# Residual loads of finished rows brought forward a tile, and the first low parts of the second pass put in front of subtractions

## The chip, the cores and the metric

The kernel runs on one core of one Trainium2 chip. Its time is the device time of one execution in microseconds (us), and the lower the better. The kernel before takes 2166.55 us, the median of three runs (2166.4 to 2170.19). In the profile the engines are PE (TensorE, matrix products; PEld is its loading of weights), DVE (VectorE), ACT (ScalarE), POOL (GpSimd) and SP (SyncE, which here issues nearly all DMA transfers).

## The reference, cut to what matters

One decoder layer is computed for 2048 prompt rows and 64 sample rows of width 1024: attention and gated linear attention side by side, an output projection, and then an MLP. The change touches the MLP alone:

```python
h = rms_norm(x, g_ffn_pre)
u = jax.nn.relu(jnp.einsum('btd,df->btf', h, w_up))      # 1024 -> 4096
f = jnp.einsum('btf,fd->btd', u * u, w_down)             # 4096 -> 1024
x = x + rms_norm(f, g_ffn_post)
```

So each row ends with a norm of `f`, a multiplication by the gain `g_ffn_post`, and the addition of the residual `x` (called `x1` in the kernel, kept in DRAM as `x1_d`).

## The kernel before

**Passes.** The MLP is worked in two passes (`sb` 0 and 1) of 1024 prompt rows each; the sample rows go with the first. A pass is first 16 "up units" (`up`, one for each 256 columns of the hidden width, `fc` 0 to 15), which leave the squared features in DRAM (`s_d`), and then the down products (`down`). Then the second pass does the same.

**Down products.** The product with `w_down` is done by a scheme of seven products in place of eight, each half as large in both directions. `DOWN_ORDER` has them as 6, 1, 5, 3, 2, 7, 4. Each product runs over 16 chunks of the hidden width, so a pass has 7 x 16 units `(p, fc)`. Sums of weights and features for the products lie ready in DRAM, in `s_d` and `t_d` (or are read from `w_down` itself).

**A unit.** A unit takes a feature tile (letter s, loaded as `rs`) and a weight tile (letter t, loaded as `rt`), 128 x 512 each. Both are split in two so that the fast matrix product keeps full precision (`split_copy`, L226 to L229): ACT copies the raw tile to a rounded high part (`o0s`, `o0t`, L228), DVE subtracts it from the raw tile and so gets the low part (`o1s`, `o1t`, L229). PE then does 12 matmuls, three for each of four row tiles: high t with high s, low t with high s, high t with low s (into banks `dn`). The unit's very first matmul needs only high parts; its second is the first that needs `o1t`.

**Places and look-ahead.** In the first pass raw tiles and parts have three places each (in the second four for the raw tiles and five for the parts). `load` issues the two raw transfers three units ahead on SP's queue; a transfer waits until the place is free, that is until DVE has made the low part of the unit three before.

**Finishing rows.** When product 2 is done, the first four row tiles of the pass (0 to 3, and in the first pass the sample rows, index 16) are complete, and `finish` works on them in small steps between the units of product 7: load the residual into the one place `x1` (SP, L2086), squares with a running sum on ACT (L2075), the reciprocal root on POOL (L218), multiplication by root and gain on DVE (L2094), addition of the residual on DVE (L2071, rows `f<-f,fx`). The store to the output follows later (`store_finished`). The next residual can only be loaded once the addition that reads the one place is done.

**Ahead of the next pass.** During product 4 of the first pass `ahead_of_up` loads and splits the first up weights of the second pass: `raw0_1_0` and `raw1_1_0` into the two places `h0` and `h1` of the pool `hs_pool`, high part `w00_1_0` on ACT (L1708), low part `w01_1_0` on DVE (L1709). The same two places carry other tiles (`hraw`) until product 3.

**The end of an up unit.** An up unit ends with three element-wise operations on its features (`st`: two subtractions and one addition), then one more addition of the last product's bank (`ue`), two activations on ACT, and the store of 1792 KB to `s_d`. In the last up unit of the second pass the first down operands are made beside these.

**What sets the order.** A scheduler puts each engine's instructions in one fixed order when the kernel is built, from the order of the code, declared dependencies and its own estimate of times; engines then run that order strictly, and an instruction that waits holds up all behind it. `tc.issue_after` places a transfer on SP's queue behind a named one; `add_manual_dep` with `NoSync` sets the order of two instructions on one engine and adds no wait.

Of the kernel before, what the change touches and what calls it, by code (L numbers as in the profile page):

```python
# [12 lines left out]
F32 = mybir.dt.float32  # L13
# [3 lines left out]
ALU = mybir.AluOpType  # L17
# [4 lines left out]
P = 128  # L22
D = 1024
# [104 lines left out]
def f32(ap):  # L128
    return ap.bitcast(F32)
# [23 lines left out]
def hybrid_step_kernel(ctx: ExitStack, tc: tile.TileContext, I, O):  # L153
    nc = tc.nc
# [9 lines left out]
    def rows(i):  # L164
        return min(P, NTOK - i * P)
# [7 lines left out]
    te, ac, dv = (InOrder(tc, engine) for engine in (nc.tensor, nc.scalar, nc.vector))  # L173

    def open_pool(name, side="left"):
        return tc.alloc_tile_pool(name=name, bufs=1, side=side, reuse_waits="tile")
# [23 lines left out]
    x1_d = [dpool.tile([rows(i), D], F32, name=f"x1_d{i}") for i in range(NTILE)]  # L200
# [25 lines left out]
    def split_copy(hi, lo, src, vector=nc.vector):  # L226

        nc.scalar.activation(hi, src, AF.Copy)  # L228
        vector.tensor_tensor(lo, src, f32(hi), op=ALU.subtract)  # L229

    def split_gained(wh, wl, raw, k):

# [475 lines left out]
    def run(products, n=None):  # L708
        deque(products if n is None else islice(products, n), 0)
# [842 lines left out]
    hs_pool = open_pool("h_s")  # L1552
# [274 lines left out]
                    stop=k == KT // 2 - 1 and u == 2, skip_group_check=True,  # L1827
                )

    next_X = []  # L1830

    def up(sb, fc, before, steps=iter(())):

# [3 lines left out]
        first, last = (sb, fc) == (0, 0), fc == NFC - 1  # L1837
# [6 lines left out]
        def s(n):  # L1844
            if not place:
                pool = keep if (sb, fc % 2) == (0, 1) else U[f"st{fc % 2}"]
                place.append(pool.tile([P, 7, BT], F32, tag="st", name=f"st_{sb}_{fc}", bufs=1))
            return place[0][:, n]
# [2 lines left out]
            up_product(sb, fc, p, {1: X, 2: X, 5: Z, 3: Z, 7: V, 4: V, 6: Y}[p])  # L1851

        def add(out, a, b, op=ALU.add):
            dv.tensor_tensor(s(out), a, b, op=op)

        def taken(p):

# [40 lines left out]
        for p in UP_FIRST if first else UP_ORDER:  # L1898
# [39 lines left out]
                ahead("s24")  # L1938
            downs(p)
            run(steps, 2)  # L1940
        add(6, s(0), s(6), ALU.subtract)
        add(5, s(3), s(6), ALU.subtract)
        add(4, s(5), s(0))
        run(features)

# [107 lines left out]
    def down_operand(sb, p, fc, which, raw):  # L2053

        name, kind = f"{'st'[which]}_{sb}_{p}_{fc}", "st"[which]
        if (sb, p, fc, which) == (0, DOWN_ORDER[0], 0, 1):
            pair = Dp["x1"].tile([P, 2, BT], F32R, tag="x1", name=f"o{name}", bufs=1)
            hi, lo = pair[:, 0], pair[:, 1]
        else:
            hi, lo = (Dp[kind + "s"].tile([P, BT], F32R, tag=f"o{u}", name=f"o{u}{name}", bufs=DOWN_LAST if sb else 3) for u in range(2))  # L2060
        split_copy(hi, lo, raw)
        return hi, lo

    turn = [0]
# [5 lines left out]
    def add(out, a, b):  # L2070
        nc.vector.tensor_tensor(out, a, b, op=ALU.add)  # L2071
# [4 lines left out]

    one, two = slice(0, 512), slice(512, D)

    finished = []

    def finish(i, fi, spread=False):

        n = rows(i)
        x1 = Dp["x1"].tile([P, D], F32, tag="x1", name=f"fx1_{i}", bufs=1)
        with tc.issue_after(latest[0].ins):
            nc.sync.dma_start(x1[:n], x1_d[i])  # L2086
        ssq = Dp["n"].tile([P, 1], F32, tag="fssq", name=f"fssq_{i}", bufs=2)
        squares(i, fi[:n], slice(0, D), ssq[:n])
        yield 1.4 if spread else 0.3
        store_finished()  # L2090
        rs = Dp["n"].tile([P, 1], F32, tag="frs", name=f"frs_{i}", bufs=2)
        rsqrt_mean(Dp["n"], rs[:n], ssq[:n], n, D)
        yield 0.3
        nc.vector.scalar_tensor_tensor(fi[:n], fi[:n], rs[:n], gpost[:n], op0=ALU.mult, op1=ALU.mult)  # L2094
        yield 1.3
        if spread and n == P:
            yield 1.4
        add(fi[:n], fi[:n], x1[:n])
        if spread:
            finished.append((i, fi))  # L2100
            return
        nc.sync.dma_start(y_rows(i), fi[:n])
        yield 1.3

    def store_finished():

        for i, fi in finished:
            with tc.issue_after(latest[0].ins):
                nc.sync.dma_start(y_rows(i), fi[: rows(i)])
        finished.clear()  # L2110
# [27 lines left out]
    latest = []  # L2138
# [69 lines left out]
    def down(sb):  # L2208
# [4 lines left out]
        parts, raws_, smp, f, todo, late = {}, {}, {}, {}, deque(), DOWN_ORDER[-1]  # L2213
# [23 lines left out]
        for n, (p, fc) in enumerate(units):  # L2237
# [6 lines left out]
            if sb == 1 and p == late and fc >= NFC - DOWN_LAST:  # L2244
# [3 lines left out]
                for j in range(4):  # L2248
                    for m in range(DOWN_LAST):
                        products(n + m, j)  # L2250
                    i = 12 + j
# [31 lines left out]
            if fc == NFC - 1:  # L2283
                gathers = [gather(sb, p, j, f, p_) for j, p_ in enumerate(banks)]
                if sam is not None and p == 1:
                    gathers.insert(1, gather_sample(p, f, sam))
                elif sam is not None:
                    todo.appendleft(gather_sample(p, f, sam))
                if (sb, p) == (0, DOWN_ORDER[-2]):
                    todo.extendleft(reversed(gathers))  # L2290
                else:
                    todo.extend(gathers)
                if p == 2:
                    if sb == 0:
                        todo.append(finish(NB, f[NB], True))
                    todo.extend(finish(i, f[i], not sb) for i in range(sb * 8, sb * 8 + 4))
                if p == 7 and sb == 1:
                    todo.extend(prepare_last(12 + j, j, f[12 + j]) for j in range(4))
# [28 lines left out]
    for sb in range(NSB):  # L2327
# [17 lines left out]
        if sb == 0:  # L2345
# [4 lines left out]
            Dp = {}  # L2350
# [48 lines left out]
```

## Time and profile before

| what | value |
|---|---|
| median of three runs | 2166.55 us (2166.4 to 2170.19) |
| span of the profiled execution | 2163.2 us |
| median less span, what lies around the span | 3.35 us |
| PE busy | 2150.4 us, 99% |
| DVE, ACT, POOL busy | 1528.9, 1220.9, 258.5 us |
| first pass, product 7 (first matmul to first of product 4) | 1451.48 to 1496.61 us |
| first down matmul of the second pass | 1849.39 us |

The page gives no time of its own for the profiled execution other than its span. Times in the trace are counted from the span's start. A timeline row has the start, the duration, the engine, the line, the operation with its output and inputs, how many were merged into the row, and in brackets how long the engine sat idle before it and what ended that. Tile names lose their numbers there: `fx` is a loaded residual (`fx1_2` and so on), `raw` an up weight tile. For a transfer the duration is only that of its issue on SP. A PE matmul's duration overlaps the next one's; what a unit costs is read from the distances of the starts.

### The profile page before, as it was taken

Reading aid. Unit: us, or ns where it says so; the run is one execution under the profiler, and the core shown is the slowest. Engines: PE = TensorE matmul, PEld = TensorE weight load, DVE = VectorE, ACT = ScalarE, POOL = GpSimd, SP = SyncE. Lnnn points to the kernel's source line nnn. Section 1 sums busy time; section 2 is a strip of 40 time slices with the busy share of each in tenths; the row PEclk is TensorE's granted clock in tenths of the full one; section 3 lists DMA queues with packets and bytes.
Section 4 is the critical chain, followed back from the end, with each engine's and each line's share of the span. In section 5 each row is a group of like instructions: output and inputs, shape, how many; then the busy total and the mean of one; then the engine's idle time right before and its main releaser. Section 6 shows DMA issues by size and latency. Waiting matters only on the chain.

```text
span 2163.2 us, 34238 instructions
## 1 busy us (share of the span) xinstructions
PE 2150.4 (99%) x11799; PEld 1864.7 (86%) x11799; DVE 1528.9 (71%) x3203; ACT 1220.9 (56%) x2625; POOL 258.5 (12%) x417
## 2 busy tenths in 40 slices
PE   9999999999999999999999999999999999999998
PEld 9999999999998888888888888887888888788887
DVE  7999868777875666988887555557766666555566
ACT  7999867566664444655555544344444445444454
POOL 4676501111111100000000000000000000000000
PEclk9999999999999999999999999999999999999999
DMA  7444241233437567777786777758544443766685
GB/s 242 159 142 149 98 117 46 75 108 123 147 124 276 188 217 227 250 259 273 259 275 219 261 244 223 230 181 266 177 170 161 151 160 125 247 203 195 195 262 186
DMA packets 241322, 411.54 MB, mean 190 GB/s; under 512 B 24876, under 2 KB 143132, under 8 KB 237036
## 3 DMA queue, kind: packets, MB, share of 16 engines
q1 hardware_dynamic: 240988, 409.08, 57.0%
q8 instruction: 93, 1.52, 0.3%
q14 instruction: 81, 0.66, 0.1%
q10 hardware_dynamic: 160, 0.27, 0.0%
HBM read 265.82 MB, written 143.99 MB: 189 GB/s over the span
## 4 chain that ended last, share of the span: by engine, by line
PE 96%; DMA 1%; DVE 1%; ACT 1%; issue 0%; DVEq 0%; SPq 0%; ACTq 0%
PE dn L142 26%; PE gproj L142 13%; PE uc L142 8%; PE uX L142 8%; PE out L1419 7%; PE proj L142 6%; PE ud L142 4%; PE ue L142 4%; PE ub L142 4%; PE sam L142 2%; PE dsam L142 1%; PE sc L142 1%; PE pT L142 1%; PE o L142 1%; PE av L142 1%; PE out L142 1%
## 5 line engine op out<-in xcount | busy, mean ns | idle before, releaser
L142 PE MATMUL dn<-o1t,o0s 128*128 128x512 f32 x892 | 348.2, 390 | 3.8 <-DVE o1t L229 3.8
L142 PE MATMUL dn<-o0t,o1s 128*128 128x512 f32 x892 | 347.8, 390 | 0.0
L142 PE MATMUL dn<-o0t,o0s 128*128 128x512 f32 x892 | 347.4, 389 | 0.3 <-DVE f L2071 0.3
L229 DVE TENSOR_TENSOR o1s<-rs,o0s 128x512 fp32r<-128x512 f32 x224 | 154.5, 691 | 223.0 <-ACT o0s L228 218.8
L228 ACT ACTIVATE o0s<-rs 128x512 fp32r<-128x512 f32 x224 | 141.2, 631 | 297.0 <-PE dn L142 262.0
L142 PE MATMUL gproj<-wg,gxh 128*128 128x384 f32 x1024 | 272.9, 342 | 0.0
L142 PEld LDWEIGHTS dn<-o1t,o0s 128*128 128x128 f32 x892 | 167.4, 188 | 41.1 <-DVE o1t L229 5.7
L142 PEld LDWEIGHTS dn<-o0t,o0s 128*128 128x128 f32 x892 | 167.5, 188 | 37.0 <-DVE f L2071 0.7
L142 ACT ACTIVATE st<-st 128x512 f32<-128x512 f32 x224 | 141.1, 630 | 100.3 <-DVE st L142 95.3
L142 PEld LDWEIGHTS dn<-o0t,o1s 128*128 128x128 f32 x892 | 167.4, 188 | 35.1
L142 PEld LDWEIGHTS gproj<-wg,gxh 128*128 128x128 f32 x1024 | 183.9, 188 | 3.5 <-issue 3.1
L142 PE MATMUL uc<-H,s 128*128 128x512 f32 x768 | 186.5, 391 | 0.0
L142 PE MATMUL gproj<-wg,gxl 128*128 128x384 f32 x576 | 185.8, 340 | 0.0
L142 PE MATMUL uX<-H,w 128*128 128x512 f32 x768 | 185.2, 390 | 0.0
L142 PEld LDWEIGHTS uX<-H,w 128*128 128x128 f32 x768 | 144.0, 188 | 30.3
L142 PEld LDWEIGHTS uc<-H,s 128*128 128x128 f32 x768 | 143.0, 188 | 30.6 <-ACT st L142 0.2
L1419 PE MATMUL out<-wo,mt 128*128 128x512 f32 x680 | 158.6, 392 | 0.0
L218 POOL TENSOR_TENSOR frs<-rs_v,half 128x1 f32<-128x1 f32 (+1 forms) x13 | 11.9, 925 | 1201.8 <-DVE rs_v L216 1201.8
L229 DVE TENSOR_TENSOR o1t<-rt,o0t 128x512 fp32r<-128x512 f32 x223 | 152.3, 685 | 3.8 <-ACT o0t L228 3.7
L1419 PEld LDWEIGHTS out<-wo,mt 128*128 128x128 f32 x680 | 126.5, 188 | 26.1
L228 ACT ACTIVATE o0t<-rt 128x512 fp32r<-128x512 f32 x223 | 137.8, 618 | 7.6 <-DMA rt<-t_d 4.9
L142 DVE TENSOR_TENSOR st<-st 128x512 f32<-128x512 f32 x160 | 110.7, 692 | 29.5 <-ACT st L142 25.2
(429 smaller groups left out, 4307.7 us busy)
## 6 DMA issues: line engine op xcount, KB each, us to landing
s_d<-st SPq DMA_DIRECT2D x32, 1792.0 KB, 8.5
rs<-s_d SPq DMA_DIRECT2D x224, 256.0 KB, 3.0
raw<-in_w_up SPq DMA_DIRECT2D x64, 512.0 KB, 4.6
rt<-t_d SPq DMA_DIRECT2D x128, 256.0 KB, 4.2
rt<-in_w_down SPq DMA_DIRECT2D x96, 256.0 KB, 3.2
t<-in_w_down SPq DMA_DIRECT2D x64, 256.0 KB, 3.7
t_d<-t SPq DMA_DIRECT2D x32, 512.0 KB, 5.7
h_d<-ht SPq DMA_DIRECT2D x8, 1280.0 KB, 7.6
```

What stands on the lines that cost most here:

```text
L142: ins = call(*a, **k)
L218: return nc.gpsimd.tensor_tensor(out, v[:n], e, op=ALU.pow)
L228: nc.scalar.activation(hi, src, AF.Copy)
L229: vector.tensor_tensor(lo, src, f32(hi), op=ALU.subtract)
L1419: te.matmul(banks[c], x, w[:, c * 512 : (c + 1) * 512], start=k + u == 0, stop=k == KT - 1 and u == len(products) - 1,)
```

## The change

It has two parts.

**Residuals.** Loading the residual becomes a function of its own, `load_x1`. Tiles 0, 1 and 3 go to the places `h0`, `h1` and `h0` of `hs_pool`, tile 2, the sample rows and all later tiles to the place `x1` as before. When product 2 of the first pass is done, residuals 0 and 1 are loaded at once; `finish` of tile 1 starts by loading residual 2, and that of tile 2 by loading residual 3. Nothing is added or left out: the same 13 loads, the same additions.

**Low parts.** `split_copy` now returns the subtraction that makes the low part, and the two subtractions at the end of the last up unit of the second pass are kept in `held`. Each of the first two weight tiles of the second pass's down products takes one of them out and declares that its own low part stands ahead of it on DVE.

```diff
@@ -226,7 +226,7 @@
     def split_copy(hi, lo, src, vector=nc.vector):
 
         nc.scalar.activation(hi, src, AF.Copy)
-        vector.tensor_tensor(lo, src, f32(hi), op=ALU.subtract)
+        return vector.tensor_tensor(lo, src, f32(hi), op=ALU.subtract)
 
     def split_gained(wh, wl, raw, k):
 
@@ -1827,7 +1827,7 @@
                     stop=k == KT // 2 - 1 and u == 2, skip_group_check=True,
                 )
 
-    next_X = []
+    next_X, held = [], []
 
     def up(sb, fc, before, steps=iter(())):
 
@@ -1851,7 +1851,7 @@
             up_product(sb, fc, p, {1: X, 2: X, 5: Z, 3: Z, 7: V, 4: V, 6: Y}[p])
 
         def add(out, a, b, op=ALU.add):
-            dv.tensor_tensor(s(out), a, b, op=op)
+            return dv.tensor_tensor(s(out), a, b, op=op)
 
         def taken(p):
 
@@ -1938,8 +1938,9 @@
                 ahead("s24")
             downs(p)
             run(steps, 2)
-        add(6, s(0), s(6), ALU.subtract)
-        add(5, s(3), s(6), ALU.subtract)
+        differences = [add(6, s(0), s(6), ALU.subtract), add(5, s(3), s(6), ALU.subtract)]
+        if sb and last:
+            held.extend(differences)
         add(4, s(5), s(0))
         run(features)
 
@@ -2058,7 +2059,10 @@
             hi, lo = pair[:, 0], pair[:, 1]
         else:
             hi, lo = (Dp[kind + "s"].tile([P, BT], F32R, tag=f"o{u}", name=f"o{u}{name}", bufs=DOWN_LAST if sb else 3) for u in range(2))
-        split_copy(hi, lo, raw)
+        low = split_copy(hi, lo, raw)
+        if sb and which and held:
+            how = mybir.DependencyInfo(mybir.DependencyClass.NoSync, mybir.DependencyReason.DATA)
+            tc.add_manual_dep(held.pop(0).ins, low.ins.name, how, reason="operand first")
         return hi, lo
 
     turn = [0]
@@ -2076,14 +2080,23 @@
 
     one, two = slice(0, 512), slice(512, D)
 
-    finished = []
+    finished, x1s = [], {}
+
+    def load_x1(i):
+
+        pool, tag = (hs_pool, "h1" if i == 1 else "h0") if i in (0, 1, 3) else (Dp["x1"], "x1")
+        x1s[i] = pool.tile([P, D], F32, tag=tag, name=f"fx1_{i}", bufs=1)
+        with tc.issue_after(latest[0].ins):
+            nc.sync.dma_start(x1s[i][: rows(i)], x1_d[i])
 
     def finish(i, fi, spread=False):
 
         n = rows(i)
-        x1 = Dp["x1"].tile([P, D], F32, tag="x1", name=f"fx1_{i}", bufs=1)
-        with tc.issue_after(latest[0].ins):
-            nc.sync.dma_start(x1[:n], x1_d[i])
+        if i not in x1s:
+            load_x1(i)
+        if i in (1, 2):
+            load_x1(i + 1)
+        x1 = x1s.pop(i)
         ssq = Dp["n"].tile([P, 1], F32, tag="fssq", name=f"fssq_{i}", bufs=2)
         squares(i, fi[:n], slice(0, D), ssq[:n])
         yield 1.4 if spread else 0.3
@@ -2292,6 +2305,8 @@
                     todo.extend(gathers)
                 if p == 2:
                     if sb == 0:
+                        load_x1(0)
+                        load_x1(1)
                         todo.append(finish(NB, f[NB], True))
                     todo.extend(finish(i, f[i], not sb) for i in range(sb * 8, sb * 8 + 4))
                 if p == 7 and sb == 1:
```

**SP, first pass, units 13 to 15 of product 7 and what follows.** In a name such as `rt_0_7_13` stand the pass, the product and the chunk; a last number only counts tiles. Before:

```order
L2050 DMA rs_0_7_13_16610<-s_d0_13_112 128x512
L2050 DMA rt_0_7_13_16612<-t_d13_144 128x512
L2086 DMA fx1_2_16635<-x1_d2_161 128x1024
L2050 DMA rs_0_7_14_16640<-s_d0_14_113 128x512
L2050 DMA rt_0_7_14_16642<-t_d14_145 128x512
L2109 DMA out_y_prompt<-f_1_14949 128x1024
L2050 DMA rs_0_7_15_16670<-s_d0_15_114 128x512
L2050 DMA rt_0_7_15_16672<-t_d15_146 128x512
L2050 DMA rs_0_4_0_16694<-s_d0_0_99 128x512
L2050 DMA rt_0_4_0_16696<-t_d0_131 128x512
L2086 DMA fx1_3_16719<-x1_d3_162 128x1024
L2050 DMA rs_0_4_1_16724<-s_d0_1_100 128x512
```

Now:

```order
L2051 DMA rs_0_7_13_16612<-s_d0_13_112 128x512
L2051 DMA rt_0_7_13_16614<-t_d13_144 128x512
L2090 DMA fx1_3_16637<-x1_d3_162 128x1024
L2051 DMA rs_0_7_14_16642<-s_d0_14_113 128x512
L2051 DMA rt_0_7_14_16644<-t_d14_145 128x512
L2122 DMA out_y_prompt<-f_1_14949 128x1024
L2051 DMA rs_0_7_15_16672<-s_d0_15_114 128x512
L2051 DMA rt_0_7_15_16674<-t_d15_146 128x512
L2051 DMA rs_0_4_0_16696<-s_d0_0_99 128x512
L2051 DMA rt_0_4_0_16698<-t_d0_131 128x512
L1704 DMA raw0_1_0_16916<-in_w_up 128x4x256
L2051 DMA rs_0_4_1_16724<-s_d0_1_100 128x512
```

The load of a residual behind `rt_0_7_13` is that of tile 3 where it was tile 2; and behind `rt_0_4_0` now stands the first up weight tile of the second pass, `raw0_1_0`, where residual 3 stood. (Before, `raw0_1_0` stood about 100 places further up, among the units of product 3, and `raw1_1_0` a little behind it; the latter now stands behind `rt_0_4_3`. Residuals 0 and 1 now stand behind `rt_0_7_2`, and residual 2 behind `rt_0_7_10`.)

**DVE, first pass, the same units.** Before:

```order
L229 TENSOR_TENSOR o1t_0_7_12_16619<-rt_0_7_12_16588,o0t_0_7_12_16618 128x512
L2071 TENSOR_TENSOR f_2_14952<-f_2_14952,fx1_2_16635 128x1024
L229 TENSOR_TENSOR o1s_0_7_13_16645<-rs_0_7_13_16610,o0s_0_7_13_16644 128x512
L229 TENSOR_TENSOR o1t_0_7_13_16649<-rt_0_7_13_16612,o0t_0_7_13_16648 128x512
L229 TENSOR_TENSOR o1s_0_7_14_16675<-rs_0_7_14_16640,o0s_0_7_14_16674 128x512
L229 TENSOR_TENSOR o1t_0_7_14_16679<-rt_0_7_14_16642,o0t_0_7_14_16678 128x512
L229 TENSOR_TENSOR o1s_0_7_15_16699<-rs_0_7_15_16670,o0s_0_7_15_16698 128x512
L229 TENSOR_TENSOR o1t_0_7_15_16703<-rt_0_7_15_16672,o0t_0_7_15_16702 128x512
L2071 TENSOR_TENSOR f_3_14983<-f_3_14983,fx1_3_16719 128x1024
L229 TENSOR_TENSOR o1s_0_4_0_16729<-rs_0_4_0_16694,o0s_0_4_0_16728 128x512
L229 TENSOR_TENSOR o1t_0_4_0_16733<-rt_0_4_0_16696,o0t_0_4_0_16732 128x512
```

Now:

```order
L229 TENSOR_TENSOR o1t_0_7_12_16621<-rt_0_7_12_16590,o0t_0_7_12_16620 128x512
L2075 TENSOR_TENSOR f_3_14983<-f_3_14983,fx1_3_16637 128x1024
L229 TENSOR_TENSOR o1s_0_7_13_16647<-rs_0_7_13_16612,o0s_0_7_13_16646 128x512
L229 TENSOR_TENSOR o1t_0_7_13_16651<-rt_0_7_13_16614,o0t_0_7_13_16650 128x512
L229 TENSOR_TENSOR o1s_0_7_14_16677<-rs_0_7_14_16642,o0s_0_7_14_16676 128x512
L229 TENSOR_TENSOR o1t_0_7_14_16681<-rt_0_7_14_16644,o0t_0_7_14_16680 128x512
L229 TENSOR_TENSOR o1s_0_7_15_16701<-rs_0_7_15_16672,o0s_0_7_15_16700 128x512
L229 TENSOR_TENSOR o1t_0_7_15_16705<-rt_0_7_15_16674,o0t_0_7_15_16704 128x512
L1709 TENSOR_TENSOR w01_1_0_16941<-raw0_1_0_16916,w00_1_0_16940 128x512
L229 TENSOR_TENSOR o1s_0_4_0_16729<-rs_0_4_0_16696,o0s_0_4_0_16728 128x512
L229 TENSOR_TENSOR o1t_0_4_0_16733<-rt_0_4_0_16698,o0t_0_4_0_16732 128x512
```

The addition behind unit 12 is that of tile 3 where it was tile 2, and behind unit 15 the low part of the up weights, `w01_1_0`, has the place of the last addition. On ACT the high part `w00_1_0` moves alike, from between units 7 and 8 to between `o0t_0_7_15` and `o0s_0_4_0`. The additions of tiles 1 and 2 now stand behind units 7 and 9 (before, tile 1 behind unit 9), and the multiplication of tile 3 moves from in front of unit 9 to behind unit 10.

**DVE, second pass, the start of the down products.** Before (`st_1_15` belongs to the last up unit, the row with `ue` adds its last product):

```order
L229 TENSOR_TENSOR o1s_1_6_2_19482<-rs_1_6_2_19453,o0s_1_6_2_19481 128x512
L229 TENSOR_TENSOR o1s_1_6_3_19506<-rs_1_6_3_19477,o0s_1_6_3_19505 128x512
L142 TENSOR_TENSOR st_1_15_19295<-st_1_15_19295 128x512 x3
L142 TENSOR_TENSOR st_1_15_19295<-st_1_15_19295,ue_1_15_19273 128x512
L229 TENSOR_TENSOR o1t_1_6_0_19462<-rt_1_6_0_19447,o0t_1_6_0_19461 128x512
L229 TENSOR_TENSOR o1t_1_6_1_19470<-rt_1_6_1_19451,o0t_1_6_1_19469 128x512
L229 TENSOR_TENSOR o1t_1_6_2_19486<-rt_1_6_2_19455,o0t_1_6_2_19485 128x512
L229 TENSOR_TENSOR o1t_1_6_3_19510<-rt_1_6_3_19479,o0t_1_6_3_19509 128x512
L142 TENSOR_TENSOR st_1_15_19295<-st_1_15_19295 128x512
L229 TENSOR_TENSOR o1s_1_6_4_19530<-rs_1_6_4_19501,o0s_1_6_4_19529 128x512
```

Now:

```order
L229 TENSOR_TENSOR o1s_1_6_2_19482<-rs_1_6_2_19453,o0s_1_6_2_19481 128x512
L229 TENSOR_TENSOR o1s_1_6_3_19506<-rs_1_6_3_19477,o0s_1_6_3_19505 128x512
L229 TENSOR_TENSOR o1t_1_6_0_19462<-rt_1_6_0_19447,o0t_1_6_0_19461 128x512
L142 TENSOR_TENSOR st_1_15_19295<-st_1_15_19295 128x512
L229 TENSOR_TENSOR o1t_1_6_1_19470<-rt_1_6_1_19451,o0t_1_6_1_19469 128x512
L142 TENSOR_TENSOR st_1_15_19295<-st_1_15_19295 128x512
L229 TENSOR_TENSOR o1t_1_6_2_19486<-rt_1_6_2_19455,o0t_1_6_2_19485 128x512
L142 TENSOR_TENSOR st_1_15_19295<-st_1_15_19295 128x512
L142 TENSOR_TENSOR st_1_15_19295<-st_1_15_19295,ue_1_15_19273 128x512
L229 TENSOR_TENSOR o1t_1_6_3_19510<-rt_1_6_3_19479,o0t_1_6_3_19509 128x512
L229 TENSOR_TENSOR o1s_1_6_4_19530<-rs_1_6_4_19501,o0s_1_6_4_19529 128x512
L229 TENSOR_TENSOR o1t_1_6_4_19534<-rt_1_6_4_19503,o0t_1_6_4_19533 128x512
```

`o1t_1_6_0` stands behind the four low parts of features and ahead of all the `st` rows; the next ones alternate with them, and the `st` row that closed the group now comes after `o1t_1_6_4`. On ACT the two last activations of `st_1_15` move back by three instructions, and on SP the store of 1792 KB moves behind the two loads for unit 8.

## The prediction

> **What bounds the kernel now.** I read the page's span and busy times first, then who PE waited for over the whole span, then PE's timeline where those waits lie, then DVE, SP and ACT at the same places.
>
> ```profile
> span 2163.2 us, 34238 instructions
> PE 2150.4 (99%) x11799; PEld 1864.7 (86%) x11799; DVE 1528.9 (71%) x3203; ACT 1220.9 (56%) x2625; POOL 258.5 (12%) x417
> ...
> PE dn L142 <- DVE o1t L229: 3.8, 4, 2.1
> PE dn L142 <- DVE f L2071: 0.3, 1, 0.3
> ```
>
> PE is busy 99% of the span, so only its gaps can be won. In the down products it waited five times in all: four times for a weight tile's low part, once for a gather that frees a bank. The idle of these rows understates the loss, since a matmul's modelled duration overlaps the next. Distances between starts tell it. In the chain that ended last a run of 1298 matmuls takes 294.53 us, so one start to the next is 0.227 us:
>
> ```profile
> 1851.88 294.53 PE dn L142 x1298
> ```
>
> The gaps, on PE's timeline of both places:
>
> ```profile
> 1478.84 0.39 PE L142 MATMUL dn<-o0t,o0s 128*128 128x512 f32 x1
> 1479.59 0.50 PE L142 MATMUL dn<-o1t,o0s 128*128 128x512 f32 x1 [0.36 <-DVE o1t L229]
> 1487.65 0.39 PE L142 MATMUL dn<-o0t,o0s 128*128 128x512 f32 x1
> 1488.55 0.50 PE L142 MATMUL dn<-o1t,o0s 128*128 128x512 f32 x1 [0.51 <-DVE o1t L229]
> 1496.61 0.39 PE L142 MATMUL dn<-o0t,o0s 128*128 128x512 f32 x1
> 1497.82 0.50 PE L142 MATMUL dn<-o1t,o0s 128*128 128x512 f32 x1 [0.82 <-DVE o1t L229]
> 1499.54 0.39 PE L142 MATMUL dn<-o0t,o1s 128*128 128x512 f32 x1
> 1500.22 0.50 PE L142 MATMUL dn<-o0t,o0s 128*128 128x512 f32 x1 [0.29 <-DVE f L2071]
> ...
> 1849.39 0.39 PE L142 MATMUL dn<-o0t,o0s 128*128 128x512 f32 x1
> 1851.88 0.50 PE L142 MATMUL dn<-o1t,o0s 128*128 128x512 f32 x1 [2.10 <-DVE o1t L229]
> 1852.22 0.39 PE L142 MATMUL dn<-o0t,o1s 128*128 128x512 f32 x1
> ```
>
> First pass: 0.52 in unit 10 of product 7, 0.67 in unit 13, 0.98 and 0.45 in unit 0 of product 4, 2.62 us together. After each gap the next start comes 0.34 later in place of 0.23 (1851.88 to 1852.22), four times 0.11: **3.05 us**. Second pass: 2.49 less 0.23, **2.26 us**. Both parts of the change aim at these; 5.3 us, 0.25% of the time, is about all there is.
>
> **Who is late in the first pass.** DVE, SP and ACT there:
>
> ```profile
> 1464.02 0.68 DVE L229 TENSOR_TENSOR o1t<-rt,o0t 128x512 fp32r<-128x512 f32 x1
> 1466.49 1.23 DVE L2071 TENSOR_TENSOR f<-f,fx 128x1024 f32<-128x1024 f32 x1 [1.80 <-DMA fx<-x_d]
> 1467.64 1.28 DVE L2094 SCALAR_TENSOR_TENSOR f<-f,frs,gfpost 128x1024 f32<-128x1024 f32 x1
> 1468.83 0.69 DVE L229 TENSOR_TENSOR o1s<-rs,o0s 128x512 fp32r<-128x512 f32 x1
> ...
> 1470.04 0.20 DVE L216 TENSOR_SCALAR rs_v<-fssq 128x1 f32<-128x1 f32 x2
> ...
> 1472.48 2.48 DVE L2094 SCALAR_TENSOR_TENSOR f<-f,frs,gfpost 128x1024 f32<-128x1024 f32 x2 [0.43 <-POOL frs L218]
> ...
> 1477.10 1.22 DVE L2071 TENSOR_TENSOR f<-f,fx 128x1024 f32<-128x1024 f32 x1 [0.94 <-DMA fx<-x_d]
> 1478.25 0.69 DVE L229 TENSOR_TENSOR o1s<-rs,o0s 128x512 fp32r<-128x512 f32 x1
> 1478.85 0.68 DVE L229 TENSOR_TENSOR o1t<-rt,o0t 128x512 fp32r<-128x512 f32 x1
> ...
> 1486.07 1.23 DVE L2071 TENSOR_TENSOR f<-f,fx 128x1024 f32<-128x1024 f32 x1 [3.56 <-DMA fx<-x_d]
> ...
> 1495.34 1.23 DVE L2071 TENSOR_TENSOR f<-f,fx 128x1024 f32<-128x1024 f32 x1 [3.92 <-DMA fx<-x_d]
> ...
> 1461.27 0.39 SPq L2086 DMA_DIRECT2D fx<-x_d  x1
> 1470.51 0.43 SPq L2086 DMA_DIRECT2D fx<-x_d  x1
> 1479.93 0.42 SPq L2086 DMA_DIRECT2D fx<-x_d  x1
> 1488.89 0.42 SPq L2086 DMA_DIRECT2D fx<-x_d  x1
> ...
> 1468.43 0.63 ACT L1708 ACTIVATE w<-raw 128x512 fp32r<-128x512 f32 x1 [2.19 <-DMA out_y_sample<-fs]
> 1468.97 0.61 ACT L228 ACTIVATE o0s<-rs 128x512 fp32r<-128x512 f32 x1
> ```
>
> Each of the four additions of a residual finds it not there, and the low parts queue behind it on DVE. From SP's issue to the addition's start: 5.22, 6.59, 6.14 and 6.45 us for tiles 0 to 3. SP issues such a load 1.08 us after the start of the low part that it queues behind (1478.85 to 1479.93), and the addition comes only two units later, about 5.4 us of PE time.
>
> **Part 1, step by step.** No instruction is added. Residuals 0 and 1 are there in time now, since they are issued behind `rt_0_7_2`, over ten us ahead of their use. But residual 2 still stands behind `rt_0_7_10` with its addition behind unit 9, and residual 3 behind `rt_0_7_13` with its addition behind unit 12: the two places of tiles 1 and 2 before. So one must follow DVE. A low part takes 0.60 from start to start (1478.25 to 1478.85), an addition 1.15 (1466.49 to 1467.64), a multiplication 1.19 (1467.64 to 1468.83).
>
> From 1464.02, with no wait for residual 0: addition 0 at 1464.62, multiplication 1 at 1465.77, low parts of unit 7 at 1466.96 and 1467.56, addition 1 at 1468.16, unit 8 at 1469.31 and 1469.91. The two small operations for the roots start at 1470.51, and the multiplication of tile 2 comes 2.44 later as before (1470.04 to 1472.48, POOL's root): 1472.95. Unit 9 at 1474.14 and 1474.74, ahead of its need at 1476.2. Residual 2 is issued at 1467.56 + 1.08 = 1468.64 and with the worst 6.59 lands at 1475.23; addition 2 is due at 1475.34, so it no longer waits. Unit 10's `o1t` starts at 1477.09 in place of 1478.85, and the gap of unit 10 goes.
>
> Residual 3 is issued at 1478.17. The nearest row, the load of 1479.93 at this very place in the queue, says 6.14: addition 3 at 1484.31, after two to three us of waiting as before. `o1t` of unit 13 starts at 1486.06; PE follows 0.74 later (1851.14 to 1851.88 below), at 1486.80. Without gaps PE needs it at 1488.55 - 0.67 - 0.73 (unit 10's gap with its restart, and 0.1 just before it), 1487.15. So this gap goes too, just.
>
> Now `raw0_1_0`. It is issued behind `rt_0_4_0`, that is at 1486.06 + 1.08 = 1487.14, and ACT, strictly in order, holds `o0s_0_4_0` and all behind it until it has landed. Before, it was loaded about 100 places earlier on SP, and ACT's copy of it waited 2.19 us (for another transfer, the row of 1468.43) between units 7 and 8, where PE did not feel it. Its landing here is not in the trace. Bounds: 4.6 us, the median of these loads, and 6.59, the slowest residual; I take 6.45, that of residual 3, which stood at this place among the same neighbours and is as large (512 KB). Then `w00_1_0` starts at 1493.59, DVE's `w01_1_0` 0.63 later at 1494.22. Before, from addition 3 (1495.34) to the bank's release on PE (1500.22) 4.88 us passed: 1.15 for the addition, four low parts 2.40, and 1.33 for the gather. Now 0.60 + 2.40 + 1.33: PE's tenth matmul of that unit starts at 1498.55. ACT keeps up, at 0.54 an operation (1468.43 to 1468.97). It started at 1500.22, and without any gap would at 1497.17. **Part 1 gives 1.67 us**, and leaves 1.4. Each us on either landing takes one us off, as long as the sum of both exceeds 11.2: both at 6.59, 1.1 us; raw at 4.6, all 3.05. Both landings depend on how full the queue is, so I go no finer. The rows for the median of the raw loads, and for the large store that part 2 moves (size, median us from issue to landing):
>
> ```profile
> s_d<-st SPq DMA_DIRECT2D x32, 1792.0 KB, 8.5
> ...
> raw<-in_w_up SPq DMA_DIRECT2D x64, 512.0 KB, 4.6
> ```
>
> [...]
>
> What costs nothing: the 1 MB of residuals 0 and 1 is issued by SP ahead of `rs_0_7_3`, two issues of 0.4 us; that tile is loaded three units, 8.2 us, ahead, and even a landing of 6.6 leaves 1.5. Were the cover gone, PE would lose what it is late. `raw1_1_0`, now behind `rt_0_4_3`, is first read three units later, 8 us.
>
> **Part 2.** DVE and ACT at the start of the second pass's down products:
>
> ```profile
> 1848.48 2.15 DVE L142 TENSOR_TENSOR st<-st 128x512 f32<-128x512 f32 x3 [0.45 <-ACT st L142]
> 1850.55 0.68 DVE L142 TENSOR_TENSOR st<-st,ue 128x512 f32<-128x512 f32 x1
> 1851.14 2.50 DVE L229 TENSOR_TENSOR o1t<-rt,o0t 128x512 fp32r<-128x512 f32 x4
> ...
> 1848.36 0.62 ACT L228 ACTIVATE o0t<-rt 128x512 fp32r<-128x512 f32 x1
> 1849.60 2.07 ACT L228 ACTIVATE o0t<-rt 128x512 fp32r<-128x512 f32 x3 [0.62 <-PE ue L142]
> ```
>
> `o0t_1_6_0` is done at 1848.98, but its low part starts at 1851.14, behind four `st` rows. Now it starts at 1849.01 and PE 0.74 later, at 1849.75 where it was 1851.88: **2.13 us**. What is late next: the other low parts, each now behind one `st` row or two (0.6 to 0.7 each). `o0t` of unit 1 can't start before 1849.60 (it waits for PE's last up product), so its low part ends by 1851.0; PE needs it at 1849.75 + 2.7 = 1852.5. Units 2 and 3 end by 1852.3 and 1854.2, wanted at 1855.2 and 1857.9. The store of 1792 KB moves behind the loads of unit 8 and goes out some 3 us later, near 1857.5; with 8.5 us it lands by 1866, and loads queued with it belong to unit 9, which PE starts at 1874. If this cover of some 6 us were gone, PE would wait in unit 9 or 10.
>
> **Sum.** 1.67 + 2.13 = 3.8 us off the span of 2163.2, so 2159.4. The median of the runs lies 3.35 above the span; this start and end are not touched: 2166.55 - 3.8 = **2162.75 us**, 0.18% less.
>
> **Rivals.** What a measurement here can tell from no change is about 0.2%, 4.33 us, or a time under 2162.2.
>
> *Both stalls gone.* If raw weights land as in the up units (4.6), part 1 gives 3.05, together 5.2: 2161.4. For it: SP's burst behind the wait for residual 3 starts 1.8 us earlier than before, and 4.6 is the median of 64. Against: hard by, four of four loads took over 5.
>
> *Part 1 gives nothing.* The waits are shifted by a tile, not removed, and the sum of landings is 14.3 or more: 2.13 alone, 2164.4. For it: the order shows the same two-unit distance. Against: 7.1 each was not seen.
>
> *Slower.* ACT's wait for `raw0_1_0` is a new one, between the parts of product 7 and those of product 4, and PE has no other work there. It decides from a landing of 8.1 us on (6.45 + 1.67; then part 1 costs), and outweighs part 2 and 4.33 us besides from 14.6 us on (6.45 + 3.8 + 4.33): 2171 or more. For it: nothing else can run on ACT meanwhile. Against: the longest row is 8.5, for 1792 KB.
>
> **Chances.** Forecast 0.47 (2162.2 to 2163.9), both gone 0.34, part 1 nothing 0.13, slower 0.06. So faster 0.34, within 0.60, slower 0.06. The range of 2161.2 to 2165.0 takes in the three cases on the fast side.
>
> **What would show it.** Right: PE's gap at the second pass's first unit under 0.3 us; no gap in units 10 and 13 of product 7; DVE waiting only for the residual of tile 3; ACT waiting for `raw0_1_0` some 5 us, and a gap of one to two us in unit 0 of product 4. Wrong: no wait of ACT for `raw`; DVE waiting for residual 2; a gap of PE in units 9 or 10 of the second pass's product 6, or in unit 3 of product 7.

## The result

The changed kernel takes 2160.69 us, median of ten runs (2159.9 to 2163.58), beside 2166.38 us of the kernel before (ten runs, 2162.45 to 2170.19). The ratio is **0.9979, interval 0.9971 to 0.9986**: 4.5 us less (3.0 to 6.3). Two later measurements of the same kernel, told below, gave 0.9989 (0.9981 to 0.9998) and 0.9982 (0.9974 to 0.9991). The mean of the three, 0.9983, is 3.6 us.

The page of the profile after, its span and PE:

```profile
span 2160.9 us, 34240 instructions
...
PE 2149.6 (99%) x11799; PEld 1864.0 (86%) x11799; DVE 1529.1 (71%) x3203; ACT 1221.6 (57%) x2625; POOL 258.5 (12%) x417
```

Whom PE waited for over the whole span (us in total, times, longest):

```profile
...
PE dn L142 <- DVE o1t L229: 0.8, 2, 0.6
PE proj L142 <- ACT wa_hi L142: 0.7, 1, 0.7
PE sc L142 <- POOL kl L468: 0.7, 2, 0.5
...
PE dn L142 <- DVE f L2075: 0.3, 1, 0.3
```

The wait for low parts has fallen from 3.8 us in four times to 0.8 in two. The rows for `wa_hi` and `kl` belong to the attention part, which no edit touches; the kernel before has neither of them in its profile. Such waits come and go between executions; here they come to 1.4 us, so that two single profiles (2163.2 and 2160.9) differ by less than the 3.6 us of gaps that went at the places changed. What is left of those gaps, on PE's timeline:

```profile
1496.49 0.39 PE L142 MATMUL dn<-o0t,o0s 128*128 128x512 f32 x1
1497.10 0.50 PE L142 MATMUL dn<-o1t,o0s 128*128 128x512 f32 x1 [0.22 <-DVE o1t L229]
...
1498.82 0.39 PE L142 MATMUL dn<-o0t,o1s 128*128 128x512 f32 x1
1499.50 0.50 PE L142 MATMUL dn<-o0t,o0s 128*128 128x512 f32 x1 [0.29 <-DVE f L2075]
...
1848.67 0.39 PE L142 MATMUL dn<-o0t,o0s 128*128 128x512 f32 x1
1849.68 0.50 PE L142 MATMUL dn<-o1t,o0s 128*128 128x512 f32 x1 [0.61 <-DVE o1t L229]
1850.01 0.40 PE L142 MATMUL dn<-o0t,o1s 128*128 128x512 f32 x1
```

The gaps in units 10 and 13 of product 7 are gone. Unit 0 of product 4 keeps 0.38 and 0.45, with the restart of 0.11 after each **1.06 us** (unrounded), where the first pass had 3.17 before (the prediction's 3.05 and 0.1 just ahead of unit 10's gap). The second pass keeps 0.78 + 0.10, **0.88 us**, where it had 2.37 (2.26 and its restart). By the gaps part 1 gave 2.1 us in this execution and part 2 gave 1.5, 3.6 together.

DVE at these places (start, duration, and in brackets how long it sat idle and for what):

```profile
1476.13 1.23 DVE L2075 TENSOR_TENSOR f<-f,fx 128x1024 f32<-128x1024 f32 x1 [0.29 <-DMA fx<-x_d]
...
1484.99 1.23 DVE L2075 TENSOR_TENSOR f<-f,fx 128x1024 f32<-128x1024 f32 x1 [2.83 <-DMA fx<-x_d]
...
1495.15 0.69 DVE L1709 TENSOR_TENSOR w<-raw,w 128x512 fp32r<-128x512 f32 x1 [4.60 <-ACT w L1708]
...
1848.93 0.69 DVE L229 TENSOR_TENSOR o1t<-rt,o0t 128x512 fp32r<-128x512 f32 x1 [1.62 <-PE ue L142]
```

Additions 0 and 1 wait for nothing, addition 2 for 0.29 us, addition 3 still for 2.83. The weights' cast is late, because ACT's own cast is. SP's issue and ACT's rows:

```profile
1478.96 0.42 SPq L2090 DMA_DIRECT2D fx<-x_d  x1
...
1487.82 0.42 SPq L1704 DMA_DIRECT2D raw<-in_w_up  x1
```

```profile
1494.49 0.63 ACT L1708 ACTIVATE w<-raw 128x512 fp32r<-128x512 f32 x1 [4.66 <-DMA raw<-in_w_up]
...
1847.63 0.62 ACT L228 ACTIVATE o0t<-rt 128x512 fp32r<-128x512 f32 x1
1848.87 1.79 ACT L228 ACTIVATE o0t<-rt 128x512 fp32r<-128x512 f32 x3 [0.63 <-PE ue L142]
```

From issue to use, residual 3 takes 6.03 us and `raw0_1_0` 6.67. And in the second pass a wait stands that the prediction did not have: the first low part's high part is done at 1848.25 (1847.63 + 0.62), but the low part starts only at 1848.93, released by PE's last up product (`ue`).

### The profile page after: what moved, and what is told of

Its sections match the earlier page's. It is cut to its first block, busy times and chain, and to the rows that moved or that the text cites. A ratio compares the mean times of both kernels' runs of the same rounds, so it can differ in the third digit from the quotient of the medians.

```text
span 2160.9 us, 34240 instructions
## 1 busy us (share of the span) xinstructions
PE 2149.6 (99%) x11799; PEld 1864.0 (86%) x11799; DVE 1529.1 (71%) x3203; ACT 1221.6 (57%) x2625; POOL 258.5 (12%) x417
## 4 chain that ended last, share of the span: by engine, by line
PE 93%; DVE 2%; ACT 2%; DMA 1%; issue 1%; POOL 0%; SPq 0%; DVEq 0%; POOLq 0%; ACTq 0%
PE dn L142 27%; PE gproj L142 13%; PE uc L142 8%; PE uX L142 8%; PE out L1419 7%; PE proj L142 6%; PE ue L142 4%; PE ud L142 4%; PE ub L142 4%; PE dsam L142 1%; PE sam L142 1%; PE o L142 1%; PE sc L142 1%; PE pT L142 1%; PE av L142 1%; PE out L142 1%
```

## Experiments

The theory: the gain is the PE gaps that are gone, part 1 and part 2 add up, the gaps left in unit 0 of product 4 come from ACT's cast of `raw0_1_0`, and the gap left in the second pass from the place of the first low part. Rivals: the gain is more than the gaps (the medians lie 5.7 us apart, the gaps give 3.6); addition 3's wait is what holds PE; the low part waits for PE's product itself, whatever its place.

| run | ratio to the kernel before | interval | gaps left, first pass | second pass |
|---|---|---|---|---|
| the kernel before | 1 | | 3.17 us | 2.37 us |
| the change, first time | 0.9979 | 0.9971 to 0.9986 | 1.06 | 0.88 |
| part1 | 0.9994 | 0.9985 to 1.0002 | 1.34 | 2.36 |
| part2 | 0.9990 | 0.9982 to 0.9999 | 2.46 | 0.88 |
| again | 0.9989 | 0.9981 to 0.9998 | 2.53 | 0.89 |
| again_2 | 0.9982 | 0.9974 to 0.9991 | 1.43 | 0.88 |
| best | 0.9977 | 0.9969 to 0.9986 | 0.54 | 0.22 |
| late_cast | 0.9977 | 0.9968 to 0.9986 | 0.69 | 0.23 |
| late_cast_early_3 | 0.9977 | 0.9968 to 0.9986 | 0 | 0.23 |
| no_gap (the same kernel) | 0.9972 | 0.9961 to 0.9984 | 0.10 | 0.24 |

The gaps are of the one profiled execution of each run, the distance between two starts less 0.23 us for each matmul, restarts included. One more run, residual_3_other_place, has a profile and a single time.

### The two parts apart, and the whole again

For part1 the order of low parts and subtractions is left as before; for part2 the residuals are:

```diff
 part1:
-        if sb and last:
-            held.extend(differences)
 part2:
-        if i in (1, 2):
-            load_x1(i + 1)
...
-                        load_x1(0)
-                        load_x1(1)
```

(in part2 every residual also has the one place `x1`, and is loaded when its own tile is finished.)

> Only the residuals loaded ahead; the second pass starts as in the kernel before. Theory (the gain is the TensorE gaps that are gone): the first pass keeps 1.05 us of its 3.17 us of gaps between 1460 and 1510 us, the second pass keeps its 2.37 us, so the time falls by 2.1 us (ratio 0.9990). Rival (the loads ahead also spare something outside these gaps, since the medians lie further apart than the gaps do): the time falls by 3 us or more.

> Only the two low parts ahead of the subtractions; the residuals are loaded as in the kernel before. Theory: the first pass keeps its 3.17 us of gaps, the second pass keeps 0.88 of 2.37 us, so the time falls by 1.5 us (ratio 0.9993). Rival: the late store of the last feature row or the later subtractions cost something in the second pass and the fall is under 1 us, or the second pass gains more than its gap and the fall is over 2 us.

> The changed kernel once more, beside its two halves on the same chip. Theory: the two parts lie 350 us apart and add up, 3.6 us below the kernel before (ratio 0.9983). Rival: the whole is worth more than the sum of its parts by over 1 us.

Measured: 1.3 us less for part 1 (interval 3.2 less to 0.4 more, so that its time alone can't be told from no change), 2.2 us for part 2 (0.2 to 3.9), 2.4 for the whole (0.4 to 4.1). The two parts add to 3.5, which lies inside the intervals of both measurements of the whole made so far (3.0 to 6.3 and 0.4 to 4.1). Part 2 is as expected in its place; its 2.2 us lie over the 2 us that its rival names, but the interval holds both. Two of its rows on PE's timeline, the gap of the second pass:

```profile
1847.37 0.39 PE L142 MATMUL dn<-o0t,o0s 128*128 128x512 f32 x1
1848.37 0.50 PE L142 MATMUL dn<-o1t,o0s 128*128 128x512 f32 x1 [0.61 <-DVE o1t L229]
```

Its first pass, with the residuals loaded as before, has 2.46 us of gaps, not 3.17: they differ between executions. The gap of unit 10 isn't there at all, although the order of loads is the old one: residual 1 took 6.05 us from its issue to its addition (1468.84 to 1474.89), where it took 6.59 before. With the change they differ more. In the run again, the very same kernel, on the timelines of PE, ACT and SP:

```profile
1494.58 0.39 PE L142 MATMUL dn<-o0t,o1s 128*128 128x512 f32 x1
1496.02 0.51 PE L142 MATMUL dn<-o0t,o0s 128*128 128x512 f32 x1 [1.05 <-ACT o0t L228]
1496.91 0.50 PE L142 MATMUL dn<-o1t,o0s 128*128 128x512 f32 x1 [0.39 <-DVE o1t L229]
```

```profile
1494.30 0.63 ACT L1708 ACTIVATE w<-raw 128x512 fp32r<-128x512 f32 x1 [5.88 <-DMA out_y_prompt<-f]
```

```profile
1486.52 0.42 SPq L1704 DMA_DIRECT2D raw<-in_w_up  x1
```

The cast starts 7.78 us after the issue, ACT waited 5.88 us, and PE stopped for 1.21 us even before the first matmul of the unit, since the high part `o0t` stood behind the cast. (The row names a store of `f` as the one that ended the wait; it was issued after `raw` on the same queue, and I can't tell the two apart here.) So against the 3.17 us of the kernel before part 1 is worth 2.1 us in one execution and 0.6 (3.17 - 2.53) in another, by how long one cast waited. Against the 2.46 us of part2 it is worth nothing in the latter.

For the size of the whole a third measurement:

> The changed kernel a third time, for the size of its gain: its two measurements so far gave ratios of 0.9979 and 0.9989, and its two profiles had gaps of 1.06 and 2.53 us left in the first pass. Theory (the gain is the gaps, and the length of the load of raw0_1_0 differs between executions): the ratio lies between 0.9979 and 0.9989, and the gaps left in the first pass are 0.5 us more for each 0.5 us that this load takes over 6.7 us. Rival (the gain is larger than the gaps): 0.9979 or less with gaps over 1 us.

It gave 0.9982, between the two others, with 1.43 us of gaps in the first pass. Its cast, on ACT's timeline:

```profile
1493.55 0.63 ACT L1708 ACTIVATE w<-raw 128x512 fp32r<-128x512 f32 x1 [4.77 <-DMA raw<-in_w_up]
```

That is 6.84 us after its issue (1486.71). Four executions with the residuals loaded ahead (part1 among them) stand side by side: from the load's issue to its cast passed 6.67, 6.84, 6.96 and 7.78 us, and the gaps were 1.06, 1.43, 1.34 and 2.53. That gaps grow with this time holds from end to end; the two in the middle are out of order by 0.1 us. Their mean is 1.6 us, and that of the two executions with the old loads (3.17 and 2.46) is 2.8: by these means part 1 gives 1.2 us, close to the 1.3 of its time.

The rival of a gain larger than the gaps has lost its ground: the mean of the three ratios is 3.6 us, as much as the gaps of the first comparison, and the 5.7 between the medians of the first measurement did not come again. But by the means above the gaps give 2.7 (1.2 + 1.5), and with intervals that reach some 1.7 us to either side an extra of a us is not excluded.

### Where the rest waits: best

```diff
+        elif sb and which:
+            pair = Dp["ts"].tile([P, 2, BT], F32R, tag="o", name=f"o{name}", bufs=DOWN_LAST)
+            hi, lo = pair[:, 0], pair[:, 1]
...
-        if i in (1, 2):
-            load_x1(i + 1)
+        if i == 1:
+            load_x1(2)
+            load_x1(3)
```

In the second pass the pool `ts` holds five places for high parts and behind them five for low ones, 2 KB each a partition. The pools `sr`, `ss` and `tr` stand below it with 8, 20 and 8 KB, so the low parts begin at 36 + 10 = 46 KB. The space is that of `hs_pool` (8 KB) and of the places of products 6, 3 and 4 of the up units (16 KB each), so all above 40 KB still belongs to what the last up product, 4, reads. With pairs the first low part lies at 38 to 40 KB.

> The changed kernel with two further edits: residual 3 is loaded together with residual 2 instead of one tile later, and in the second pass high and low part of a down operand share one place, so that the first low part lies beside its high part instead of in space that TensorE's last up product still reads. Theory: addition 3 no longer waits (2.83 us now), the first up weights of the second pass are issued near 1485 us instead of 1487.8, ScalarE waits for them 2 us less, and the 1.05 us of gaps in unit 0 of product 4 are gone; in the second pass the first low part starts at the end of its high part, 0.7 us earlier, and the gap of 0.88 us falls under 0.2. Together 1.7 us below the changed kernel, 5.3 below the kernel before (ratio 0.9975). Rival for the first pass: two residuals of 512 KB on one queue land later together, addition 2 waits 2 us or more instead and a gap opens in units 9 to 11 of product 7. Rival for the second pass: the gap stays, since it is TensorE's own last product and not the place that the low part waited for.

The second pass came out as the theory said. On DVE's timeline, and below on PE's:

```profile
1848.64 0.69 DVE L229 TENSOR_TENSOR ot<-rt,ot 128x512 fp32r<-128x512 f32 x1 [0.97 <-ACT ot L228]
```

```profile
1849.04 0.85 PE L142 MATMUL dn<-ot,o0s 128*128 128x512 f32 x2
1849.72 0.40 PE L142 MATMUL dn<-ot,o1s 128*128 128x512 f32 x1
```

The low part now waits for its own high part, not for PE, starts ahead of the end of PE's last up product and leaves 0.22 us of gap, about the 0.2 expected. So it was the place.

The first pass went half as expected. On DVE's and ACT's timelines:

```profile
1477.92 1.23 DVE L2078 TENSOR_TENSOR f<-f,fx 128x1024 f32<-128x1024 f32 x1 [1.22 <-DMA fx<-x_d]
...
1481.59 1.23 DVE L2078 TENSOR_TENSOR f<-f,fx 128x1024 f32<-128x1024 f32 x1
```

```profile
1494.53 0.63 ACT L1708 ACTIVATE w<-raw 128x512 fp32r<-128x512 f32 x1 [2.87 <-DMA raw<-in_w_up]
```

Addition 3 no longer waits, addition 2 waits 1.22 us, and no gap of 0.2 us opens in product 7. But `raw0_1_0` was issued at 1487.97, not near 1485. Addition 3, whose place it takes, had started over six us earlier, so it isn't that place that set its issue; SP issued the loads ahead of it one after the other until then (the last three at 1485.40, 1486.47 and 1487.47). The 1.06 us of gaps fell to 0.35, not to nothing, with 0.18 new in unit 11 of product 7.

### The cast itself: late_cast and late_cast_early_3

The cast of `raw0_1_0` on ACT gets an order behind the cast of the third weight tile of product 4, by the same kind of dependency that part 2 uses:

```diff
...
-        low = split_copy(hi, lo, raw)
+        high, low = split_copy(hi, lo, raw)
+        if (sb, p, fc, which) == (0, DOWN_ORDER[-1], 2, 1):
+            anchor.append(high)
...
-            split_by(scalar, vector, *parts, src)
+            first = split_by(scalar, vector, *parts, src)
+            if anchor:
...
+                tc.add_manual_dep(first.ins, anchor.pop().ins.name, how, reason="operand first")
```

> The changed kernel with the shared place for the second pass's low parts (as in the run best, whose earlier load of residual 3 is not taken), and with ScalarE's cast of raw0_1_0 put behind its cast of the third down operand of product 4, where it stood in front of the first one; its load is issued where it was. Theory (the gaps left in unit 0 of product 4 come from ScalarE's cast of raw0_1_0, which waited 4.7, 5.3 and 5.9 us in three executions for loads that took 6.7, 7.0 and 7.8 us, with gaps of 1.06, 1.34 and 2.53 us): the cast now asks for its data some 5 us later and waits under 1 us, no gap is left in units 0 and 1 of product 4, and the bank gap of 0.56 us goes too, since VectorE's sums are no longer held; with the second pass's gap at 0.2 the time falls 5.2 us below the kernel before (ratio 0.9976), whatever addition 3 waits. Rival 1 (addition 3's wait of 2.8 us also holds TensorE): a gap of 0.3 us or more stays in units 13 of product 7 to 1 of product 4. Rival 2 (the up weights are needed there): the gap moves to units 3 to 5 of product 4 or to the start of the second pass's up products.

> The same with residual 3 loaded together with residual 2, as in the run best. Theory: addition 3's wait is covered in any case, so that nothing is won over the run late_cast (within 0.5 us; the small gap of 0.18 us in unit 11 of product 7 that the run best had may come back, since addition 2 waited 1.2 us there). Rival: the earlier load of residual 3 is what took the gap from 1.06 to 0.35 us in the run best, and this kernel is faster by 0.7 us than late_cast.

(Both kernels have the run best's place for the low parts too, which acts in the second pass alone.)

In late_cast the cast waits no more, and the second matmul of unit 0 follows at once. Nor did the wait move to later units, as rival 2 had it: over the whole profile PE waits for a down operand or bank once, and never for an up weight. But the gap for the bank stays. On the timelines of ACT, SP and PE:

```profile
1496.03 0.63 ACT L228 ACTIVATE o0s<-rs 128x512 fp32r<-128x512 f32 x1 [3.02 <-DMA rs<-s_d]
...
1499.83 0.61 ACT L1708 ACTIVATE w<-raw 128x512 fp32r<-128x512 f32 x1
```

```profile
1489.03 0.45 SPq L2055 DMA_DIRECT2D rs<-s_d  x1
```

```profile
1498.49 0.39 PE L142 MATMUL dn<-o0t,o1s 128*128 128x512 f32 x1
1499.31 0.50 PE L142 MATMUL dn<-o0t,o0s 128*128 128x512 f32 x1 [0.43 <-DVE f L2084]
```

Behind `raw0_1_0` SP had issued the operand `rs` of unit 1, and that one is now what is late: 7.0 us from issue to use for 256 KB. DVE's low parts of that unit come late with it, and behind them the sums that free the bank: 0.59 + 0.10. My statement that this gap would go was wrong; rival 1 named it (a gap of over 0.3 us stays), and late_cast_early_3 shows that addition 3's wait has a share: with residual 3 loaded earlier, no gap is left. That is against its theory, by which nothing was to be won. PE's busy time over 30 us there (start and end, length, busy time of each engine with its instructions, clock, DMA share, GB/s), first of the change and then of late_cast_early_3:

```profile
1470.00:1500.00 30.00, 29.48 (x129) 23.82 (x128) 21.08 (x33) 12.81 (x22) 1.05 (x2) 1.00 0.86 280
```

```profile
1470.00:1500.00 30.00, 30.00 (x134) 24.83 (x133) 22.76 (x34) 13.97 (x24) 1.05 (x2) 1.00 0.93 313
```

The times of the two can't be told apart (both 0.9977; medians 2160.76 and 2160.03): 0.7 us is less than the intervals are wide.

### The place of residual 3

```diff
-(hs_pool, "h1" if i == 1 else "h0")
+(hs_pool, "h0" if i == 0 else "h1")
```

> The changed kernel with residual 3 in the place of residual 1 instead of that of residual 0, so that raw0_1_0's place is free after addition 0, and its load is issued some 19 us earlier, in front of unit 10's operands of product 7; the casts of it on ScalarE and VectorE stand as much earlier, in front of those of unit 9. Theory (what costs is that the casts stand in the queues nearer to the load's issue than the 6 to 7 us that it takes): the wait does not go but moves, ScalarE waits 4 us or more for raw0_1_0 near 1470 us and a gap of 1 to 3 us opens in units 9 or 10 of product 7, while units 0 and 1 of product 4 have none. Rival (the gap came from the place that was taken): no wait of over 1 us and no gap in either place, 1 us below the changed kernel.

Both were wrong in part. SP issued `raw0_1_0` at 1467.22, and ACT's cast waited for it:

```profile
1472.44 0.63 ACT L1708 ACTIVATE w<-raw 128x512 fp32r<-128x512 f32 x1 [2.12 <-DMA raw<-in_w_up]
```

The wait moved, as the theory said, but it is 2.12 us and not 4 or more (the load took 5.22), and no gap opens: the parts of units 9 and 10 were far enough ahead. Unit 0 of product 4 has no gap for a low part; the one for the bank stays, with 0.60 + 0.11. What stands ahead of it is the same as before: `raw1_1_0`, which now has to wait for residual 3's place, went out where `raw0_1_0` had stood, and the operand `rs` of unit 1 behind it again took 7.03 us from issue to use. On the timelines of SP and ACT:

```profile
1488.21 0.43 SPq L1704 DMA_DIRECT2D raw<-in_w_up  x1
1488.73 0.46 SPq L2051 DMA_DIRECT2D rs<-s_d  x1
```

```profile
1495.76 0.63 ACT L228 ACTIVATE o0s<-rs 128x512 fp32r<-128x512 f32 x1 [2.95 <-DMA rs<-s_d]
```

A single time of 2162.27 us says nothing of so little.

### The version without gaps, beside the change

> The run late_cast_early_3 beside the changed kernel on the same chip. Theory: its first pass has no gap whatever the load takes, and 0.23 us is left in the second pass; the time lies 1.7 to 3 us below that of the changed kernel of this call (ratio to the kernel before 0.9975). Rival: the two can't be told apart, under 1 us.

On the same chip no_gap takes 2158.14 us (ratio 0.9972, 0.9961 to 0.9984) and the changed kernel 2162.28 (0.9982, 0.9974 to 0.9991). The medians are 4.1 us apart, the gaps only 1.43 + 0.88 - 0.10 - 0.24 = 2.0; the intervals overlap. In no_gap's profile PE waits for no `dn` operand at all. It also lacks two waits that the changed kernel's profile has elsewhere, 0.9 us for `kl` of the attention part and 0.3 us for DVE's `samq`; such waits come and go, and no run puts them down to these edits. No_gap is the fastest of these kernels by the medians.

## Why the prediction was right, and where it was not

**The time.** 2162.75 us was forecast, 3.8 us less than before; the ratio of the first measurement makes it 4.5 (2162.0 on the scale of the 2166.55 shown), and the mean of three 3.6 (2162.9): inside the range, and near the forecast. The fall is 0.21% by the first ratio, at the bound of what can be told from no change, and 0.17% by the three, within it, as was held likeliest. The first median itself, 2160.69, lies 0.5 under the range: in each measurement the medians of one kernel moved by a us or more (the kernel before: 2166.38, 2165.6, 2164.82, 2165.76; the change: 2160.69, 2163.49, 2162.28). The working made one mistake with such a move: it set the span of one execution against the median of others and found 3.35 us around the span. The profiled execution after has its own time, 2162.71, and lies 1.8 above its span. The difference of 3.8 did not depend on it.

**Part 1, mechanism.** Right in all steps but one: residuals 0 and 1 cost nothing, residual 3 waits (2.83 us, "two to three"; landing 6.03, forecast 6.14), units 10 and 13 have no gap, ACT waits for `raw0_1_0` and a gap is left in unit 0 of product 4, and moving the cast (late_cast) took away what hung on it. The step that was wrong: addition 2 was not to wait, and DVE waiting for residual 2 was named as a sign of being wrong; it waited 0.29 us here and 0.25, 0.73 and 0.80 in the three other executions. The working let the multiplication of tile 2 come 2.44 us after the small operations for the roots, "as before". But in that stretch stood three low parts, 1.8 us, one of which the change moves away and two of which the sum had already counted ahead of it; POOL's roots, for which DVE still waited 0.43 us behind them, took 2.62 us there. Now DVE is idle meanwhile, POOL takes 1.05 us for the same two roots, and the rows follow 0.87 us apart (why POOL is quicker no run tried by itself):

```profile
1472.48 0.21 DVE L216 TENSOR_SCALAR rs_v<-fssq 128x1 f32<-128x1 f32 x2
1473.35 1.28 DVE L2107 SCALAR_TENSOR_TENSOR f<-f,frs,gfpost 128x1024 f32<-128x1024 f32 x1 [0.66 <-POOL frs L218]
```

So addition 2 was due earlier than forecast, and waited for its residual. Not forecast either was a wait of 0.44 us for POOL's root before the multiplication of tile 1. PE felt none of this.

**Part 1, size.** The term that decided was the landing of `raw0_1_0`, taken as 6.45 from residual 3's row. To the start of the cast it was 6.67, 6.84, 6.96 and 7.78, and the gap left, forecast as 1.4, was 1.06, 1.43, 1.34 and 2.53. The forecast lies in the middle, but it was given as one number with "no finer" where four executions spread by 1.5 us, almost the whole worth of part 1. In the rival *slower*, where the landing decides from 8.1 us on, one of four came within 0.4 us of that point; with part 2 beside it the kernel is still not slower. What was held against this rival, "the longest row is 8.5", misread the page of the profile: its figures are medians. The trace of the kernel before has landings from 3.9 to 9.5 us for the 512 KB loads of `raw`, the longest at 691 us, far from here.

The rival *both stalls gone* rested on the 4.6 us of the raw loads, and it fell: all four took 6.67 us or more. The Trainium skill's page "DMA: Bandwidth & Descriptors", section "Anatomy of one DMA", fits the transfers that GpSimd issues as 2.0 us plus bytes over 436 GB/s, an estimate of 3.2 us for 512 KB. SP issues the loads here, so that fit is not for them, and they took twice as long or more. The rival *part 1 gives nothing* is less clearly out. Unit 13's gap (0.67 and 0.68 us in the two executions with the old loads, restarts aside) went in all four; unit 10's went too, but part2 had none either. Three of the four have less of gaps than both executions with the old loads, the fourth (2.53) lies between those two, and the interval of part 1's time alone takes in no gain at all.

**Part 2.** The step that failed is "it starts at 1849.01": the low part was taken to be free as soon as its high part is done. Its place was not free. It lies in space that PE's last up product reads, and so 0.78 us of the gap of 2.26 stayed (the prediction's first sign, a gap under 0.3 us, failed); with restarts counted the part gave 1.49 us (2.37 - 0.88) in place of 2.13. The row that should have told it stood in the prediction: ACT's next high parts wait for `ue`, for the same space, and what holds them could hold the low part too. Before the change the four `st` rows hid this. The run best put the place elsewhere and the 0.66 went. The rest of part 2 came as forecast: no gap for the other low parts, and none in units 9 and 10 behind the later store.

**The sum.** 1.67 + 2.13 = 3.8 was forecast; 2.1 + 1.5 = 3.6 in the first profile, 1.3 and 2.2 by the times of the parts alone with intervals of some 3.6 us each. The two errors, part 1 forecast too small there and part 2 too large, nearly cancel. That the total came so close is in part luck: in the run again the gaps that went are 0.6 + 1.5 = 2.1.

## What to carry to other kernels

When the cause of a stall is taken away, look for the next thing that the same instruction needs, its place too: a row that waits for freed space a few operations further on is the sign. An operation that waits for a transfer on an engine in strict order should stand as far behind the transfer's issue as the longest landing measured in that stretch, not the median of the kernel; putting one cast three units later cost nothing and took its wait away. And when such a wait goes, the transfer queued behind it is the next one late: late_cast kept 0.69 us of gap until residual 3 moved too.

## What the runs showed of the hardware

A 512 KB load into the same place took 5.2 us to its use (residual_3_other_place, issued at 1467) and 6.7 to 7.8 us (issued at 1486 to 1488; at the longest the profile names another transfer as the one waited for), and ten such loads in the up units from 1540 to 1620 us of the changed kernel had a median of 4.0; a 256 KB load right behind one took 7.0 us to its use, where the median of the 224 in the kernel is 3.0. The change's profile by stretches, first where `raw0_1_0` was under way, then in two up units (the last two numbers are the DMA engines' busy share and GB/s):

```profile
1487.80:1494.50 6.70, 6.70 (x32) 5.53 (x31) 2.20 (x4) 1.28 (x3) 0.00 (x0) 1.00 0.89 272
...
1565.00:1573.00 8.00, 8.00 (x36) 6.52 (x35) 7.38 (x11) 3.30 (x5) 0.00 (x0) 1.00 0.66 246
1600.00:1608.00 8.00, 8.00 (x36) 6.49 (x35) 6.01 (x9) 3.86 (x6) 0.00 (x0) 1.00 0.38 121
```

The slow loads fall where the engines are 0.89 busy. That fits a queue shared with the operands' loads and the rows' stores, but fewer bytes beside the load were not tried on their own, so the cause of its length, and of its spread of 1.1 us between executions of one kernel, stays open.
